# A two-layer hybrid encoder on one core: S5 parameters made once, the second layer's S5 tables moved into the first feed-forward stage, and reciprocal roots on GpSimd

## Chip, core and metric

One Trainium2 chip, one of its cores. The metric is the device time of one execution, in microseconds. TensorE multiplies matrices into PSUM; VectorE (DVE), ScalarE (ACT) and GpSimd (POOL) do elementwise work, each with its own in-order queue; SyncE (SP) and ScalarE issue the transfers.

## The reference, cut to what matters

The input is 512 positions of 1024 channels. Each of two layers runs three token mixers in parallel on the normalized input (differential attention with 8 heads, a 2-D Fourier mix, a bidirectional S5 state-space layer), gates and merges them, and goes on with a gated feed-forward of width 2816 and a gated per-layer embedding (PLE).

```python
def rms_norm(x, g):
    y = xf * lax.rsqrt(jnp.mean(xf * xf, axis=-1, keepdims=True) + EPS)
    return y * g
def s5_mix(u, a_re, a_im, log_dt, b_re, b_im, c_re, c_im, d):
    ...
    for direction in range(2):
        lam = lax.complex(a_re[direction], a_im[direction])
        dt = jnp.exp(log_dt[direction])[:, None]
        a_bar = jnp.exp(lam * dt)
        b_scale = (a_bar - 1.0) / lam
        _, xs = lax.associative_scan(_ssm_combine, (a_elems, bu * b_scale), axis=1,
                                     reverse=(direction == 1))
        state = state + xs
    y = jnp.einsum('bsgp,ghp->bsgh', state, c_mat).real
```

There are 32 S5 groups of 16 channels with 64 complex states each, and the parameters (a, dt, b, c) depend on the weights alone, not on x.

## The kernel before, in words

Activations lie with channels on the 128 partitions and all 512 positions in the free dimension, so a tile is 128x512. Each f32 product is made of three matmuls on split operands: `unit` loads 512 KB of weights (two buffers `wr`), ScalarE makes the high parts `wh` (line 94), VectorE the low parts `wl` by subtraction (line 95), six buffers each, and `mm` (line 106) runs high-high, high-low and low-high. A unit of 1024 columns gives 24 matmuls. Results go into the PSUM banks "w" (three), "s" (two), "t", "o" and "m" (one each).

The program is written as a list of tile operations; a planner orders them on each engine when the kernel is built. An operation written earlier goes first among those that are ready; `high_priority(offset=-LOW)` puts what is in it 600 places later. The order is then fixed, and each engine goes through its queue in order.

A layer runs: the norm; `s5_params`; `s5_load_u` (S5 input, stored to DRAM); `fourier`; eight heads of attention (v in pairs, q and k with rotary, `head`), with `s5_tables` for the eight chunks of four S5 groups written between the heads; `s5_toeplitz`; then the gather of U from DRAM, `s5_chunk` for eight chunks among the gates and branch projections, `s5_out`, the GLU, w_out; the norm and the feed-forward (22 pairs of units up, eight rows down); the norm and PLE.

`s5_params` (line 277 on) makes the powers of the discretized pole, the scaled inputs and the phase tables for one layer's 64 columns (2 directions x 32 groups); 144 instructions on VectorE and 24 on GpSimd, and leaves them in SBUF (Wr, Wi, BWr, BWi and phases). `s5_tables` makes from them, for one chunk: products `tb` on GpSimd (lines 400, 401, 417, 418, and complex products at lines 238 to 243), an addition on VectorE (402, 419), 16 matmuls with `cat` (410), two ScalarE copies behind each pair of them into `vbt` and `kfb` (411, 412), and six stores to the DRAM table `tab` (413, 420, 435, 438). Buffers are few: `tb1` has two, `tb2`, `bc` and `vbt` one. `s5_toeplitz` lays `kfb` out in the DRAM table `dtab`.

`rsqrt` (line 109) makes 1/sqrt by a bit trick and three Newton steps: eight small VectorE instructions on 128x4 values. It stands behind every norm and behind every head (`rms`), where a matmul with the result (line 146) follows.

Of the kernel before, what the change touches and what calls it, by code (L numbers as in the profile page):

```python
# [50 lines left out]
class Kernel:  # L51
# [57 lines left out]
    def rsqrt(self, pool, v, n):  # L109

        nc = self.nc
# [91 lines left out]
    def exp_acc(self, pool, out, x, n, V):  # L203
        k = self.t(pool, "ex1", (P, 64))[:, :n]
        r = self.t(pool, "ex2", (P, 64))[:, :n]
        q = self.t(pool, "ex3", (P, 64))[:, :n]
# [39 lines left out]
    def setup(self):  # L246
# [8 lines left out]
        nc.vector.memset(self.ones, 1.0)  # L255
        self.cst = self.t(self.cp, "cst", (P, 3))
# [17 lines left out]
    def s5_params(self, i, keep, pool, R):  # L274
        nc, a = self.nc, self.a
        V = nc.vector
        n = 64
# [5 lines left out]
        nc.sync.dma_start(prm, a["s5p"][i])  # L283
# [18 lines left out]
        Wr = self.t(keep, "Wr", (P, 8, n))  # L302
        Wi = self.t(keep, "Wi", (P, 8, n))
        Br = self.t(keep, "BWr", (P, 8, n))
        Bi = self.t(keep, "BWi", (P, 8, n))
        V.tensor_tensor(out=Wr[:, 0], in0=r1, in1=c, op=ALU.mult)
        V.tensor_tensor(out=Wi[:, 0], in0=r1, in1=sn, op=ALU.mult)
# [6 lines left out]
        V.tensor_scalar(out=nr, in0=Wr[:, 0], scalar1=-1.0, scalar2=None, op0=ALU.add)  # L314
        V.tensor_tensor(out=t, in0=nr, in1=are, op=ALU.mult)
        V.tensor_tensor(out=u, in0=Wi[:, 0], in1=aim, op=ALU.mult)
        V.tensor_tensor(out=t, in0=t, in1=u, op=ALU.add)
        V.tensor_tensor(out=Br[:, 0], in0=t, in1=den, op=ALU.mult)
        V.tensor_tensor(out=t, in0=Wi[:, 0], in1=are, op=ALU.mult)
        V.tensor_tensor(out=u, in0=nr, in1=aim, op=ALU.mult)  # L320
        V.tensor_tensor(out=t, in0=t, in1=u, op=ALU.subtract)
        V.tensor_tensor(out=Bi[:, 0], in0=t, in1=den, op=ALU.mult)

        tmp = self.t(pool, "ptmp", (P, 7, n))
        G = nc.gpsimd
        for w in (1, 2, 4):
            self.cmul(G, Wr[:, w:2 * w], Wi[:, w:2 * w], Wr[:, 0:w], Wi[:, 0:w],
                      Wr[:, w - 1:w].to_broadcast([P, w, n]), Wi[:, w - 1:w].to_broadcast([P, w, n]), tmp[:, 0:w])
        self.cmul(G, Br[:, 1:8], Bi[:, 1:8], Wr[:, 0:7], Wi[:, 0:7],
                  Br[:, 0:1].to_broadcast([P, 7, n]), Bi[:, 0:1].to_broadcast([P, 7, n]), tmp)  # L330
# [12 lines left out]

        ph = []
        for q in range(2):
            co = self.t(keep, f"phc{q}", (P, n, 8))
            si = self.t(keep, f"phs{q}", (P, n, 8))
            V.memset(co[:, :, 0:1], 1.0)
            V.memset(si[:, :, 0:1], 0.0)
            f = [c8, s8] if q == 0 else [fc, fs]  # L350
            k = 1
            while True:
                b = [P, n, k]
                self.cmul(V, co[:, :, k:2 * k], si[:, :, k:2 * k], co[:, :, 0:k], si[:, :, 0:k],
                          f[0].unsqueeze(2).to_broadcast(b), f[1].unsqueeze(2).to_broadcast(b),
                          tmp.rearrange("p k n -> p (k n)")[:, :n * k].rearrange("p (n k) -> p n k", k=k))
                k *= 2
                nf = [self.t(pool, f"pf{q}{k}c", (P, n)), self.t(pool, f"pf{q}{k}s", (P, n))]
# [5 lines left out]
                if k == 8:  # L364
                    break
            fc, fs = f
            ph.append((co, si))
# [3 lines left out]
        return dict(Wr=Wr, Wi=Wi, Br=Br, Bi=Bi, ph=ph)  # L371

    def s5_tables(self, i, pool, prm, ch, kfb, cat, tab, prio):
# [5 lines left out]
        nc.sync.dma_start(bc, a["s5bc"][i, ch])  # L379

# [7 lines left out]
        def wsel(w, d, rev):  # L388
            v = w.rearrange("p k (d g) -> p d g k", d=2)[:, d, g0:g0 + GC]
            if rev:  # L390
                v = v[:, :, ::-1]
            return v.unsqueeze(3).to_broadcast(full)
# [4 lines left out]
        for d in range(2):  # L397
            vb = self.t(pool, "tb1", full, bufs=2)
            t2 = self.t(pool, "tb2", full, bufs=1)
            G.tensor_tensor(out=vb, in0=wsel(prm["Br"], d, d == 0), in1=bsel(0), op=ALU.mult)  # L400
# [349 lines left out]
    def layer(self, i, x):  # L750
# [12 lines left out]
        self.xp.release()  # L763

        self.op = self.pool(f"o{i}", side="right")
        gp = self.pool(f"gen{i}", side="right")
        rp = self.pool(f"r{i}")
        cosr = self.t(rp, "cosr")
        sinr = self.t(rp, "sinr")
# [450 lines left out]
```

## Time and profile before

| what | value |
|---|---|
| median of 3 runs | 2235.33 us (2235.26 to 2237.52) |
| the profiled execution's own time | 2237.99 us |
| its span, first to last instruction | 2236.2 us |
| mean granted TensorE clock | 0.983 |
| TensorE matmul busy | 2121.7 us (95%) |
| VectorE busy | 1534.3 us (69%) |
| ScalarE busy | 1023.5 us (46%) |
| GpSimd busy | 760.2 us (34%) |

Busy time is the union of an engine's instructions. Matmuls are pipelined, and their ends are modelled, so a busy TensorE is not one at full pace. In time, layer 1's attention lies at about 110 to 446 us, its feed-forward at 720 to 1075 us, PLE to 1135 us; layer 2's Fourier part begins near 1150 us and its attention ends near 1546 us.

### The profile page before, as it was taken

Reading aid. Unit: us, or ns where it says so; the run is one execution under the profiler, and the core shown is the slowest. Engines: PE = TensorE matmul, PEld = TensorE weight load, DVE = VectorE, ACT = ScalarE, POOL = GpSimd, SP = SyncE. Lnnn points to the kernel's source line nnn. Section 1 sums busy time; section 2 is a strip of 40 time slices with the busy share of each in tenths; the row PEclk is TensorE's granted clock in tenths of the full one; section 3 lists DMA queues with packets and bytes.
Section 4 is the critical chain, followed back from the end, with each engine's and each line's share of the span. In section 5 each row is a group of like instructions: output and inputs, shape, how many; then the busy total and the mean of one; then the engine's idle time right before and its main releaser. Section 6 shows DMA issues by size and latency. Waiting matters only on the chain.

```text
span 2236.2 us, 29074 instructions
## 1 busy us (share of the span) xinstructions
PE 2121.7 (95%) x10432; PEld 1772.2 (79%) x10432; DVE 1534.3 (69%) x2664; ACT 1023.5 (46%) x1900; POOL 760.2 (34%) x748
## 2 busy tenths in 40 slices
PE   7888989899999999999998898898999999999998
PEld 5777778688888888888887787687888888888886
DVE  7988997566666766633689899984666667665344
ACT  4256665244434444433442766552445444444333
POOL 4497876223101322200025967841330012221000
PEclk9999999999999999999998999999999999999999
DMA  5232232665323333233432322236743323333341
GB/s 186 79 110 78 86 101 97 190 222 197 116 94 95 97 102 95 92 95 97 149 118 80 105 87 90 97 123 186 259 150 107 97 90 101 97 95 96 95 130 57
DMA packets 117232, 259.20 MB, mean 116 GB/s; under 512 B 43456, under 2 KB 49856, under 8 KB 115040
## 3 DMA queue, kind: packets, MB, share of 16 engines
q1 hardware_dynamic: 87040, 218.48, 31.3%
q10 hardware_dynamic: 30048, 38.87, 5.2%
q8 instruction: 82, 1.34, 0.3%
q14 instruction: 62, 0.51, 0.1%
HBM read 216.87 MB, written 40.37 MB: 115 GB/s over the span
## 4 chain that ended last, share of the span: by engine, by line
PE 69%; DVE 13%; POOL 6%; DMA 5%; ACT 3%; issue 2%; ACTq 0%; SPq 0%; DVEq 0%; POOLq 0%
PE w L106 55%; PE s L106 5%; DVE wl L95 2%; DMA tab<-tb 1%; PE s L639 1%; DVE mx L541 1%; DMA U<-usd 1%; PE w L1079 1%; POOL ra L501 1%; POOL tb L417 1%; DVE tb L402 1%; DVE pr L553 1%; PE w L1026 1%; PE w L1028 1%; PE w L1027 1%
## 5 line engine op out<-in xcount | busy, mean ns | idle before, releaser
L95 DVE TENSOR_TENSOR wl<-wr,wh 128x512 fp32r<-128x512 f32 x596 | 465.5, 785 | 303.5 <-ACT wh L94 295.6
L94 ACT ACTIVATE wh<-wr 128x512 fp32r<-128x512 f32 x596 | 368.5, 624 | 631.4 <-PE w L106 424.7
L106 PE MATMUL w<-hh,wh 128*128 128x512 f32 x1536 | 607.8, 396 | 20.1 <-DVE rs L499 9.0
L106 PE MATMUL w<-hl,wh 128*128 128x512 f32 x1536 | 604.8, 394 | 2.3 <-DVE hl L82 2.2
L106 PE MATMUL w<-hh,wl 128*128 128x512 f32 x1536 | 604.6, 394 | 1.6 <-DVE wl L95 1.6
L106 PEld LDWEIGHTS w<-hh,wh 128*128 128x128 f32 x1536 | 291.6, 190 | 82.5 <-DVE rs L499 10.6
L106 PEld LDWEIGHTS w<-hl,wh 128*128 128x128 f32 x1536 | 291.2, 190 | 63.5 <-DVE hl L82 5.0
L106 PEld LDWEIGHTS w<-hh,wl 128*128 128x128 f32 x1536 | 290.9, 189 | 62.0 <-DVE wl L95 2.2
L180 POOL TENSOR_TENSOR sq<-sq,sq 128x512 f32<-128x512 f32 x18 | 25.0, 1391 | 454.0 <-ACT sq L178 454.0
L191 POOL TENSOR_TENSOR ge<-ge,cv 128x512 f32<-128x512 f32 x44 | 57.8, 1315 | 305.3 <-DVE ge L190 305.3
L106 PE MATMUL w<-ah,wl 128*128 128x512 f32 x352 | 140.4, 399 | 0.0
L106 PE MATMUL w<-al,wh 128*128 128x512 f32 x352 | 138.7, 394 | 0.0
L106 PE MATMUL w<-ah,wh 128*128 128x512 f32 x352 | 138.0, 392 | 0.0
L546 ACT ACTIVATE pr<-s,mx 128x512 f32<-128x512 f32 x128 | 87.9, 689 | 54.5 <-DVE mx L541 49.2
L541 DVE TENSOR_REDUCE mx<-s 128x1 f32<-128x512 f32 x128 | 85.7, 678 | 8.9 <-PE s L540 8.9
L936 POOL TENSOR_TENSOR uu<-uu,cv 128x512 f32<-128x512 f32 x44 | 58.2, 1323 | 71.9 <-DVE cv L193 71.9
L106 PEld LDWEIGHTS w<-al,wh 128*128 128x128 f32 x352 | 66.1, 188 | 17.1
L539 PE MATMUL s<-ks,qs 128*128 128x512 f32 x128 | 56.9, 450 | 23.7 <-ACT pr L546 23.0
L106 PEld LDWEIGHTS w<-ah,wh 128*128 128x128 f32 x352 | 66.1, 188 | 15.8
L106 PEld LDWEIGHTS w<-ah,wl 128*128 128x128 f32 x352 | 66.1, 188 | 15.3
L106 PE MATMUL w<-oh,wh 128*128 128x512 f32 x128 | 52.6, 421 | 14.8 <-DVE m L841 6.5
L553 DVE SCALAR_TENSOR_TENSOR pr<-pr,c,pr 128x512 f32<-128x512 f32 x64 | 65.8, 1028 | 1.0
(417 smaller groups left out, 4227.3 us busy)
## 6 DMA issues: line engine op xcount, KB each, us to landing
wr<-in_w_in SPq DMA_DIRECT2D x112, 512.0 KB
wr<-in_w_up SPq DMA_DIRECT2D x88, 512.0 KB
tb<-tab SPq DMA_DIRECT2D x16, 1536.0 KB
tab<-tb ACTq DMA_DIRECT2D x64, 256.0 KB
wr<-in_w_down SPq DMA_DIRECT2D x32, 512.0 KB
tab<-vbt ACTq DMA_DIRECT2D x32, 256.0 KB
wr<-in_w_attn SPq DMA_DIRECT2D x16, 512.0 KB
wr<-in_w_glu SPq DMA_DIRECT2D x16, 512.0 KB
```

Of the source, the lines that this page charges most:

```text
L94: nc.scalar.activation(hi[:, :n], raw[:, c:c + n], AF.Copy)
L95: nc.vector.tensor_tensor(out=lo[:, :n], in0=raw[:, c:c + n], in1=hi[:, :n].bitcast(F32), op=ALU.subtract)
L106: nc.tensor.matmul(ps, lhsT=w[i][a], rhs=b[i], start=start and i == 0 and q == 0, stop=stop and i == n - 1 and q == 2)
L180: eng.tensor_tensor(out=sq, in0=sq, in1=acc[c], op=ALU.add)
L191: nc.gpsimd.tensor_tensor(out=sq, in0=sq, in1=y, op=ALU.mult)
L402: nc.vector.tensor_tensor(out=vb, in0=vb, in1=t2, op=ALU.add)
L417: G.tensor_tensor(out=ct, in0=wsel(prm["Wr"], d, d == 1), in1=bsel(2), op=ALU.mult)
L539: nc.tensor.matmul(s, lhsT=q[:, c, qs], rhs=kk[:, c], start=True, stop=False)
L541: V.tensor_reduce(mx[:, c:c + 1], s, op=ALU.max, axis=AX.X, negate=True)
L546: nc.scalar.activation(pt, ss[c], AF.Exp, bias=mx[:, c:c + 1], accum_out=(s1, s2)[c][:, qt:qt + 1])
L553: V.scalar_tensor_tensor(out=pr[0], in0=pr[1], scalar=c2, in1=pr[0], op0=ALU.mult, op1=ALU.add)
L936: G.tensor_tensor(out=u, in0=u, in1=c, op=ALU.mult)
```

## The change

The parameters of both layers are made in one call, on 128 columns, in layer 1 only, behind `fourier` instead of ahead of `s5_load_u`. They no longer stay in SBUF: 16 transfers store them to the DRAM tile `par` (one piece per layer and chunk, 256 KB), and `s5_tables` loads its piece into a tile `pt` with one buffer. Layer 1's tables are written one chunk per head, 0 to 7 (before: 0 and 1 at the first head, then one ahead, none at the last). Layer 2's tables are written into the first layer's feed-forward, one chunk at each odd step 1 to 15, and its Toeplitz part behind the feed-forward. The transposed copies `vt` share the buffer of tag `tb2`. `rsqrt` becomes one GpSimd power of -0.5; the last norm of the output keeps the steps under the name `rsqrt_steps`. The host hands over the parameters in a new column order.

```diff
     def rsqrt(self, pool, v, n):
 
+        y = self.t(pool, "rsq", (P, 4), bufs=4)[:, :n]
+        self.nc.gpsimd.tensor_tensor(out=y, in0=v, in1=self.mhalf[:, :n], op=ALU.pow)
+        return y
+
+    def rsqrt_steps(self, pool, v, n):
+
...
-    def s5_params(self, i, keep, pool, R):
+    def s5_params(self, pool, R, par):
...
-        n = 64
+        n = 2 * NC
...
-        nc.sync.dma_start(prm, a["s5p"][i])
+        nc.sync.dma_start(prm, a["s5p"])
...
+        tab = self.t(pool, "ptab", (P, 8, n, 8))
+        Wr, Wi, Br, Bi = (tab[:, q] for q in range(4))
...
+        for q, v in ((0, w0r), (1, w0i), (2, b0r), (3, b0i)):
+            V.tensor_scalar(out=tab[:, q, :, 0], in0=v, scalar1=1.0, scalar2=None, op0=ALU.mult)
...
-        return dict(Wr=Wr, Wi=Wi, Br=Br, Bi=Bi, ph=ph)
-
-    def s5_tables(self, i, pool, prm, ch, kfb, cat, tab, prio):
+        for q in range(L * NCH):
+            nc.sync.dma_start(par[q], tab[:, :, q * 2 * GC:(q + 1) * 2 * GC].rearrange("p k n x -> p k (n x)"))
+
+    def s5_tables(self, i, pool, ch, kfb, cat, tab, prio):
...
+        prm = self.t(pool, "pt", (P, 8, 2, GC, 8))
+        nc.sync.dma_start(prm.rearrange("p k d g x -> p k (d g x)"), self.par[i * NCH + ch])
...
-                vt = self.t(pool, "vbt", (P, GC, P), bufs=1)
+                vt = self.t(pool, "tb2", (P, GC, P), bufs=1)
...
+    def s5_step(self, i, ch):
+        pool, kfb, cat = self.gen
+        with self.tc.high_priority(offset=-LOW):
+            self.s5_tables(i, pool, ch, kfb, cat, self.tabs[ch], self.tc.tile_snap_priority() - LOW)
...
-        tp = self.pool(f"tmp{i}")
-        prm = self.s5_params(i, gp, tp, s5R)
         fd = self.t(self.dp, "fd", (P, 4, T))
         fp = self.pool(f"four{i}")
         self.s5_load_u(i, up, hh, hl, rb, usd)
         self.fourier(i, fp, hh, hl, rb, fd)
         fp.release()
-        tp.release()
         up.release()
+        if i == 0:
+            self.s5R = self.t(self.cp, "s5R", (P, 2 * NC))
+            self.par = self.t(self.dp, "par", (L * NCH, P, 8, 2 * GC * 8))
+            tp = self.pool(f"tmp{i}")
+            self.s5_params(tp, self.s5R, self.par)
+            tp.release()
+            self.s5_begin(0, "right")
...
-            with tc.high_priority(offset=-LOW):
-                for ch in ([0, 1] if h == 0 else [h + 1] if h < 7 else []):
-                    self.s5_tables(i, gp, prm, ch, kfb, cat, tabs[ch], tc.tile_snap_priority() - LOW)
+            if i == 0:
+                self.s5_step(0, h)
...
         hh, hl, rc, rb = self.norm(x, V_GFFN)
+        if i + 1 < L:
+            self.s5_begin(i + 1, "left")
...
+            if i + 1 < L and f % 2 and f < 2 * NCH:
+                self.s5_step(i + 1, f // 2)
...
         ff.release()
+        if i + 1 < L:
+            self.s5_end(i + 1)
```

`s5_begin` allocates the pool, `kfb`, `cat` and the DRAM tables, and fills the identity part of `cat`; `s5_end` calls `s5_toeplitz` and releases the pool.

## Rows read from the trace of the kernel before

**Rows 1.** Stretches: length, busy of PE, PEld, DVE, ACT, POOL, clock, DMA, GB/s
```profile
110.00:446.00 336.00, 300.06 (x1638) 253.71 (x1636) 274.61 (x474) 182.85 (x393) 227.82 (x226) 0.96 0.35 110
446.00:720.00 274.00, 273.27 (x1358) 229.31 (x1359) 172.44 (x254) 123.05 (x204) 46.96 (x44) 1.00 0.47 146
720.00:962.00 242.00, 242.00 (x1067) 199.95 (x1066) 162.03 (x245) 113.61 (x179) 57.99 (x44) 1.00 0.31 97
962.00:1075.00 113.00, 113.00 (x489) 91.09 (x487) 42.84 (x71) 37.22 (x63) 5.28 (x9) 1.00 0.35 104
1150.00:1200.00 50.00, 39.36 (x216) 34.92 (x215) 46.64 (x139) 11.22 (x31) 25.20 (x35) 0.86 0.25 82
1150.00:1546.00 396.00, 351.20 (x1952) 301.45 (x1950) 330.87 (x643) 199.90 (x438) 253.17 (x263) 0.96 0.34 107
```

**Rows 2.** Matmuls by line, 1150 to 1546 us: first, tables', last group
```profile
L106 PE MATMUL w<-hh,wh 128*128 128x512 f32 x218 | 88.0, 404 | 3.9 <-DVE rs L499 3.9
...
L410 PE MATMUL m<-cat,tb 128*128 128x144 f32 x128 | 21.9, 295 | 4.9 <-DVE tb L402 4.0 <-ACT kfb L412 0.9
...
L132 PE MATMUL t<-ones,osb 128*128 128x1 f32 x8 | 1.0, 229 | 0.0
```

**Rows 3.** Chain that ended last, in time: start, us, what, count of instructions
```profile
455.45 1.73 PE s L639 x16
...
719.53 353.64 PE w L106 x1543
...
1197.57 3.11 PE w L1079 x26
```

**Rows 4.** One VectorE product of the S5 parameters, layer 1 (ns min/median/max)
```profile
L288 DVE TENSOR_TENSOR p_li<-prm,p_dt x1: 218/218/218, 60.6 to 60.6; 128x64 f32<-128x64 f32 x1
```

**Rows 5.** VectorE on roots, 1150:1546: temporary nww, line 117, line 115
```profile
1150.00:1546.00 396.00, 22.39 (x48) 0.96 0.34 107
1150.00:1546.00 396.00, 3.46 (x8) 0.96 0.34 107
1150.00:1546.00 396.00, 3.83 (x8) 0.96 0.34 107
```

**Rows 6.** Table buffer: PE, PEld, DVE, POOL in 1150:1546; line 402's additions
```profile
1150.00:1546.00 396.00, 21.93 (x128) 19.49 (x128) 36.34 (x35) 159.37 (x168) 0.96 0.34 107
...
L402 DVE TENSOR_TENSOR tb<-tb,tb x32: 670/684/1783, 99.9 to 1487.7; 128x512 f32<-128x512 f32 x32
```

**Rows 7.** Timeline of ScalarE behind the gather of U, layer 1
```profile
446.02 1.15 ACT L94 ACTIVATE wh<-wr 128x512 fp32r<-128x512 f32 x2 [12.42 <-DMA U<-usd]
```

**Rows 8.** VectorE, line 95 alone: stretch, length, busy us (count), clock, DMA
```profile
110.00:446.00 336.00, 50.29 (x50) 0.96 0.35 110
...
720.00:962.00 242.00, 63.93 (x90) 1.00 0.31 97
```

**Rows 9.** First table product and last table step of chunks, layer 1
```profile
L400 POOL TENSOR_TENSOR tb<-BWr,bc x16: 1098/1558/1647, 85.0 to 383.1; 128x512 f32<-128x512 f32 x16
L437 POOL TENSOR_SCALAR tb<-tb,cst x8: 691/692/1075, 149.3 to 417.4; 128x512 f32<-128x512 f32 x8
```

**Rows 10.** Waits of 110 to 446 us: us in total, times, longest
```profile
ACT pr L546 <- DVE mx L541: 27.2, 21, 5.6
POOL tb L417 <- PE m L410: 25.5, 6, 6.9
...
POOL tb L417 <- DMA tab<-tb: 11.0, 5, 4.4
```

**Rows 11.** Layer 1's S5 results, GLU matmuls, gelu split: first, last start
```profile
L668 ACT ACTIVATE ye<-t x8: 365/384/386, 475.3 to 563.4; 128x256 f32<-128x256 f32 x8
...
L106 PE MATMUL s<-soh,wh x64: 387/394/398, 612.3 to 660.8; 128*128 128x512 f32 x64
...
L82 DVE SCALAR_TENSOR_TENSOR sol<-yg,soh x4: 1096/1097/1114, 579.5 to 602.1; 128x512 fp32r<-128x512 f32 x4
```

**Rows 12.** A small GpSimd instruction in the timeline
```profile
1319.34 0.24 POOL L384 TENSOR_SCALAR bc<-bc 128x64 f32<-128x64 f32 x1 [1.80 <-DMA bc<-in_s5bc]
```

More of the change, by code (lines that the diff above doesn't have):

```diff
@@ L301, in s5_params @@
         unit(c, sn)
[L302 to L307, printed above, removed]
+        tab = self.t(pool, "ptab", (P, 8, n, 8))
+        Wr, Wi, Br, Bi = (tab[:, q] for q in range(4))
+        w0r, w0i, b0r, b0i = s("w0r"), s("w0i"), s("b0r"), s("b0i")
+        V.tensor_tensor(out=w0r, in0=r1, in1=c, op=ALU.mult)
+        V.tensor_tensor(out=w0i, in0=r1, in1=sn, op=ALU.mult)
         den, nr = s("den"), s("nr")
@@ L342, in s5_params @@
         unit(c8, s8)
-        ph = []
+        f = [c8, s8]
+        tv = self.t(pool, "ptmv", (P, n, 4))
         for q in range(2):
-            co = self.t(keep, f"phc{q}", (P, n, 8))
-            si = self.t(keep, f"phs{q}", (P, n, 8))
+            co, si = tab[:, 4 + 2 * q], tab[:, 5 + 2 * q]
             V.memset(co[:, :, 0:1], 1.0)
             V.memset(si[:, :, 0:1], 0.0)
-            f = [c8, s8] if q == 0 else [fc, fs]
-            k = 1
-            while True:
+            for k in (1, 2, 4):
                 b = [P, n, k]
                 self.cmul(V, co[:, :, k:2 * k], si[:, :, k:2 * k], co[:, :, 0:k], si[:, :, 0:k],
[L355 to L358, printed above, removed]
+                          f[0].unsqueeze(2).to_broadcast(b), f[1].unsqueeze(2).to_broadcast(b), tv[:, :, 0:k])
+                nf = [self.t(pool, f"pf{k}c", (P, n)), self.t(pool, f"pf{k}s", (P, n))]
                 V.tensor_tensor(out=t, in0=f[0], in1=f[0], op=ALU.mult)
@@ L426, in s5_tables @@
         for d in range(2):
-            lo = [x.rearrange("p (d g) k -> p d g k", d=2)[:, d, g0:g0 + GC].unsqueeze(2).to_broadcast(full)
-                  for x in prm["ph"][0]]
-            hi = [x.rearrange("p (d g) k -> p d g k", d=2)[:, d, g0:g0 + GC].unsqueeze(3).to_broadcast(full)
-                  for x in prm["ph"][1]]
+            lo = [prm[:, q, d].unsqueeze(2).to_broadcast(full) for q in (4, 5)]
+            hi = [prm[:, q, d].unsqueeze(3).to_broadcast(full) for q in (6, 7)]
             t2 = self.t(pool, "tb2", (P, 512), bufs=1)[:, 0:256].rearrange("p (g a b) -> p g a b", g=GC, a=8)
@@ L438, in s5_tables, with s5_begin, s5_end @@
         nc.scalar.dma_start(tab[:, 2560:3072], si)
+    def s5_begin(self, i, side):
+        pool = self.pool(f"gen{i}", side=side)
+        kfb = self.t(pool, "kfb", (P, 2, NG, 16))
+        cat = self.t(pool, "cat", (P, GC, W1))
+        self.nc.scalar.activation(cat[:, :, :P], self.ident.unsqueeze(1).to_broadcast([P, GC, P]), AF.Copy)
+        self.tabs = [self.t(self.dp, f"tab{ch}", (P, 3072)) for ch in range(NCH)]
+        self.dtab = self.t(self.dp, "dtab", (P, 8, NG, 16))
+        self.gen = pool, kfb, cat
+    def s5_step(self, i, ch):
+        pool, kfb, cat = self.gen
+        with self.tc.high_priority(offset=-LOW):
+            self.s5_tables(i, pool, ch, kfb, cat, self.tabs[ch], self.tc.tile_snap_priority() - LOW)
+    def s5_end(self, i):
+        pool, kfb, _ = self.gen
+        self.s5_toeplitz(i, pool, kfb, self.dtab)
+        pool.release()
     def s5_toeplitz(self, i, pool, kfb, dtab):
@@ L780, in layer @@
         tp.release()
-        tabs = [self.t(self.dp, f"tab{ch}", (P, 3072)) for ch in range(NCH)]
-        dtab = self.t(self.dp, "dtab", (P, 8, NG, 16))
         usd = self.t(self.dp, "usd", (T, T))
         ysd = self.t(self.dp, "ysd", (P, NG * NC))
-        s5R = self.t(rp, "s5R", (P, 64))
-        tp = self.pool(f"tmp{i}")
-        prm = self.s5_params(i, gp, tp, s5R)
         fd = self.t(self.dp, "fd", (P, 4, T))
@@ L1047, in ple_last @@
                 V.scalar_tensor_tensor(out=evs[tt], in0=ss, scalar=1.0 / D, in1=evs[tt], op0=ALU.mult, op1=ALU.add)
-                rs = self.rsqrt(self.small, evs[tt], 1)
+                rs = self.rsqrt_steps(self.small, evs[tt], 1)
                 x0 = xt[:, tt, 0:512]
```

65 lines of the change are left out of this document (29 added, 36 removed).

## The prediction

> **What bounds the kernel now.** I read the busy times stage by stage first. From 446 to 1075 us TensorE is busy almost without a break, with VectorE at 63 and 67% and then 38% [rows 1]; there only TensorE's own work counts. In the attention of both layers it is otherwise: 110 to 446 us and 1150 to 1546 us, where VectorE is busy 275 of 336 and 331 of 396 us, and TensorE has pauses [rows 1].
>
> "Busy" hides part of the pauses, so I count TensorE's work in layer 2's stretch. The list of matmuls by line for 1150 to 1546 us has 29 groups, of which the first, the last and the tables' own stand here [rows 2]; by columns they are 892 of 512, 636 of 256 or 258, 128 of 144 and 296 of 128 or fewer. Where nothing stops TensorE, the chain of waits gives 353.64/1543 = 229 ns for 512 columns, 3.11/26 = 120 ns for 256 and 1.73/16 = 108 ns for 64 [rows 3]; I put 144 columns between the last two, at 115 ns. Full pace: 204 + 76 + 15 + 32 = 327 us. So of 396 us 69 are stall. The same stretch has a granted clock of 0.96, and of 0.86 in its first 50 us [rows 1]: a part of the 69 us is half clock behind pauses. That is what a lighter VectorE can give back in layer 2.
>
> **Layer 2's attention: what leaves it.** Three VectorE loads go.
> The S5 parameters: 144 VectorE instructions by my count of the function, most near the 218 ns of a 128x64 product [rows 4], some longer beside GpSimd; 144 x 0.24 = 35 us, crowded into the 50 us in which VectorE is busy 46.6 [rows 1].
> The reciprocal roots: eight heads of eight instructions. Six of the eight go by one temporary, 48 instructions in 22.4 us; the two others take 3.8 and 3.5 us [rows 5]; together 30 us.
> The tables: 32 additions. The rows of the table buffer show 35 instructions in 36.3 us, of which three belong to the S5 stage [rows 6]; 34 us.
> Sum 99 us: VectorE falls from 331 to about 232 us. Tables on GpSimd go too (159 us of 253) and 128 matmuls (15 us).
>
> TensorE's floor becomes 327 - 15 = 312 us. How much stall stays? If the share of stall (69 of 396) stayed, the stretch would take 312/0.83 = 377 us, a gain of 19; with none, 312, a gain of 84. VectorE would be at 232/334 = 69%, nearest to the rows at 63 and 67% without pauses, so I take a value near the lower stall, 22 us: among it the gather of U, which held ScalarE for 12.4 us in layer 1 and which nothing in the diff touches [rows 7]. Layer 2: 396 - 334 = **62 us saved**.
>
> **The first feed-forward stage: what enters it.** TensorE has no pause there, so its 128 matmuls (15 us) are paid in full. The rest must fit beside the feed-forward work: GpSimd 159 us, VectorE 34 us, 32 pairs of ScalarE copies, per chunk two loads and six stores, and at the end the 15 stores that lay out the Toeplitz part, with ScalarE at 114 of 242 us [rows 1]. Over 720 to 1075 us GpSimd has 63 us of its own work [rows 1], so the room is there, 355 us for 159.
> VectorE is the doubtful one. A weight subtraction took 63.93/90 = 0.71 us here and 50.29/50 = 1.01 us in layer 1's attention, where GpSimd was busy 68% of the time [rows 1, 8]. If the tables were all made before 962 us, the 90 subtractions would take 27 us more, 66 other two-input instructions perhaps 10, so 162 + 34 + 37 = 233 of 257 us, 91%, more than the 84% that went with 17% of stall in layer 2's attention. That is the upper bound: 17% of 257 = 44 us. The lower is 0. The code splits weights up to three units (6 high and 6 low buffers, 24 matmuls or 5.5 us a unit) ahead of TensorE and has three banks, which attention's score chain lacks, and tables may run on below 962 us, where VectorE is at 38%. I take 7. **22 us lost.**
> The Trainium skill, page "GPSIMD Engine Reference", section "Key points", says that GpSimd shares its SBUF interfaces with VectorE and that instructions with two SBUF inputs contend with it. By that rule the FFN's subtractions would slow towards attention's 1.01 us and the sum would move towards the 44 us; taking the FFN's own 0.71 us it stays at 0. The trace agrees as far as those two rows go.
>
> **Layer 1.** Here nothing leaves but the roots. It has 30 us less VectorE work on its 275; at layer 2's rate (62 us for 99 us of VectorE and 15 of TensorE) that would be worth 15 us. But the order of the tables changes, and they decide when S5 can end.
> Before, the parameters ran beside the Fourier work, the first table product started at 85.0 us, chunks ended from 149.3 to 417.4 us, one each 38.3 us, back to back [rows 9]: a chain that waits for itself (25.5 us for its matmuls to free a buffer, 11.0 us for a store [rows 10]), not for the heads. After it came the S5 chunks (last result 563.4 us), the gelu splits (last at 602.1) and the GLU matmuls from 612.3 us [rows 11]: a margin of 10 us, with other matmuls filling until then.
> After: the parameters stand behind Fourier, in memory that Fourier uses. One row of 128 columns instead of 64 costs (670 - 218)/448 = 1.0 ns a column more, 65 ns [rows 4, 6], so 144 x 65 ns = 9 us, phases and copies some 8 more: 35 + 17 = 52 us of VectorE in one chain, drawn out to some 65 us by attention's own instructions between. I set Fourier's end at about 80 us: the first table product stood at 85.0 while Fourier and the parameters shared VectorE [rows 9]. Then come 16 stores and a load through DRAM, two waits of about 3 us (11.0/5 = 2.2 us was the mean wait for a store [rows 10]). 80 + 65 + 6: I put the first table product at 150 us.
> Per chunk, the parameter tile has one buffer and its last reader is the chunk's last step, so the next load (some 3 us) stands open; and the transposed copies now share the scratch buffer of the second product, so the next second product waits for matmuls, copies and store, for which 25.5/6 = 4.3 us was the mean wait [rows 10]; I put 5 us. Period 38.3 + 8 = 46 us. Eight chunks: 150 + 370 = 520, less some 20 when the heads have ended and the engines are free: 500, some 80 us later than 417.
> What of that reaches the end? Before, the chunks had to wait for U until 446 us, 28 us after the last table; that wait lies beside the tables now. About 55 us remain. The S5 stage itself took 446 to 563 us, sharing transfers at 146 GB/s with weights [rows 1]; with two table loads and their first half done ahead I take 25 us off. 55 - 25 - 10 of margin = **20 us lost**. Lower bound: chain hidden, relief paid, 15 gained; upper: nothing made up but the margin, 70 lost.
> The 16 stores go through SP's queue, which also brings the weights: 16 of 256 KB in 256-byte pieces. Weights behind them wait; three split units (16 us) cover it, without them up to the 20 us that I already count.
>
> **The power operation.** No row has one. Nearest is a GpSimd instruction of 128x64 at 0.24 us [rows 12]; above I set the 3.7 us of a chain that it replaces (30/8). Eight heads: 2 to 30 us of GpSimd, on the 94 us or fewer that are left in layer 2 [rows 1, 6], so nothing; in layer 1 it stands among the table products in GpSimd's queue: 0 to 30 us within the upper bound above. I take 0.3 us. It makes GpSimd wait for VectorE's variance, with rotary and table products queued behind it, whose matmuls then wait; VectorE's own queue is free of it. The norms ahead of feed-forward and PLE lie in stretches without pauses: nothing. The last root keeps its steps.
> Of the small edits (one load of parameters instead of two, roots of one buffer, the column order on the host) none lies on a path that sets the end: nothing.
>
> **Sum.** -62 + 22 + 20 = -20 us on the profiled execution's 2238.0 (its span is 2236.2): 2218. That execution lies 2.7 us above the median, so on the median 2235.3 it is **2215 us**.
>
> **Rivals.**
> A, as summed: 2215, chance 0.46, own range 2195 to 2230.
> B, layer 1's tables are hidden: gates and two projections after attention are long enough, and the relief pays 15 us. 2235 - 62 + 22 - 15 = 2180. For it: VectorE and GpSimd are free after 446 us [rows 1]; against it the 10 us of margin. 0.22.
> C, the other side: layer 1's GLU waits for its tables. Place: the first GLU matmul, 612.3 us before. Each us later costs one; from 40 us later the gains are gone. At 70, 2235 - 62 + 22 + 70 = 2265. For it the back-to-back chain; against it that chunks after attention run faster. 0.14.
> D, contention in the feed-forward stage: 44 us in place of 7, 2252. VectorE is at 91%, and late table products hold the in-order queues of VectorE and TensorE [rows 8]; the rule above says the same. Against it the three units of lead. 0.09.
> E, the change doesn't free layer 2: heads are bound by their own chain of scores, maximum, exponential and transposes, and only 19 us come back. 2258. For it, the exponential's wait for the maximum, 27.2 us in layer 1 [rows 10]; against it, VectorE makes the maximum, and it is VectorE that is freed. 0.09.
>
> **Range and chances.** About 0.2% (4.5 us) is what a measurement tells from none. Faster: B and nearly all of A (0.43), 0.65; within: 0.06, half from A's upper edge and half from milder forms of D and E; slower: the rest of C, D and E, 0.29. The range leaves out half of C and the outer ends of B, D and E, 0.2 in all: 2170 to 2262.
>
> **What would show it.** Right: 1150 to 1546 us shrinks to about 335 with VectorE near 70%; 720 to 1075 grows by 15 to 25 us; layer 1's GLU starts 10 to 40 us later than 612 with a pause of TensorE ahead of it. Wrong: a GLU start before 612 (B) or after 650 (C); subtractions near 1 us and pauses in the feed-forward stage (D); pauses in layer 2's heads as before (E).

## The result and the profile after

The change made the kernel slower: 2349.29 us (median of 4 runs, 2344.51 to 2351.04) against 2236.07 us for the kernel before beside it, a ratio of 1.0502 (95% interval 1.0484 to 1.052). The profiled execution took 2344.51 us, with a span of 2342.6 us; before, the span was 2236.2. So 106 us are to be found.

The page's busy times of the changed kernel: engine, us, share, instructions.

```profile
PE 2126.8 (91%) x10432; PEld 1777.9 (76%) x10432; DVE 1481.8 (63%) x2349; ACT 1016.6 (43%) x1895; POOL 778.8 (33%) x746
```

TensorE is busy 5 us longer than before (2121.7), and VectorE has 52 us less to do. So 101 of the 106 us are pauses of TensorE. A count by landmarks says where they lie (first GLU matmul, first result of the up half, first and last matmul of the down half, layer 2's first GLU matmul):

| stretch | before | after | change |
|---|---|---|---|
| start to layer 1's GLU | 612 | 732 | +120 |
| GLU and w_out to the up half | 107 | 106 | -1 |
| up half of feed-forward 1 | 224 | 258 | +34 |
| down half | 122 | 129 | +7 |
| down half to layer 2's GLU | 648 | 595 | -53 |
| layer 2's GLU to the end | 523 | 523 | 0 |

The feed-forward's 41 us and layer 2's 53 leave a gain of 12. Layer 1 loses 120. Such a landmark is good to some 7 us: the profiled execution was the fastest of its four, and in four runs below that leave layer 1 as it is in the changed kernel, layer 1's GLU starts at 734.7 to 739.2 us, not at 732.2.

Stretches of the changed kernel, columns as in [rows 1]: layer 1's start, the end of its tables behind the heads, the up and down halves, PLE and layer 2 up to its heads, and layer 2's heads.

```profile
110.00:150.00 40.00, 0.11 (x1) 0.14 (x1) 39.23 (x77) 0.00 (x0) 17.21 (x11) 0.50 0.00 1
...
503.00:550.00 47.00, 22.18 (x79) 17.33 (x80) 10.43 (x14) 4.43 (x13) 19.17 (x26) 0.64 0.66 169
838.00:1096.00 258.00, 241.67 (x1074) 199.64 (x1073) 210.04 (x250) 109.43 (x207) 160.44 (x141) 0.97 0.38 116
1096.00:1225.00 129.00, 127.91 (x566) 103.09 (x565) 57.61 (x78) 38.46 (x78) 58.95 (x67) 1.00 0.45 138
1225.00:1414.00 189.00, 174.73 (x913) 149.44 (x912) 114.30 (x195) 84.02 (x164) 52.55 (x54) 0.95 0.41 130
1414.00:1622.00 208.00, 202.48 (x1171) 174.62 (x1170) 160.68 (x306) 139.47 (x277) 54.72 (x39) 1.00 0.19 59
```

The first row is the surprise: for 40 us VectorE works without a break (39.23 us), GpSimd for 17.21 us, and TensorE does nothing. After the heads (second row) every engine is half idle or more, and the granted clock falls to 0.64. The last row is what the change was to do: layer 2's heads at 97% of TensorE (202.48 of 208) with VectorE at 77%.

Waits of the changed kernel from 85 to 175 us: who waited for what, us in all, times, longest.

```profile
ACT vh L81 <- DMA par<-ptab: 73.8, 1, 73.8
...
PE w L106 <- DVE rs L522: 58.6, 1, 58.6
POOL kz L825 <- DMA par<-ptab: 42.5, 1, 42.5
...
DVE vl L82 <- DMA pt<-par: 20.8, 1, 20.8
...
PE w L106 <- DVE vl L82: 14.6, 1, 14.6
```

Two things hold attention here, and TensorE pauses 58.6 + 14.6 us. From the timelines of VectorE and ScalarE:

```profile
147.80 0.69 DVE L249 TENSOR_TENSOR ptab<-ptab,ptmv 128x512 f32<-128x512 f32 x1
148.41 0.68 DVE L521 TENSOR_TENSOR ra<-w,cosr 128x512 f32<-128x512 f32 x1
...
170.06 0.47 ACT L81 ACTIVATE vh<-w,rsq 128x256 fp32r<-128x256 f32 x1 [73.78 <-DMA par<-ptab]
```

The pause of 58.6 us ends when VectorE comes to the first rotary steps (`ra`, then `rs`), right behind the last step of the parameters: VectorE's queue was full of the parameters until then, and the stores had only begun. Attention's own first tiles, `vh` and `kz`, wait longer, until 170 us, for a store of the parameters. Nothing in the computation links them. They lie in the memory that the parameters' pool has just given back, so they can be written only when the last of the 16 stores has read `ptab`. That costs TensorE the 14.6 us (for `vl` the profile names the load behind the stores), and the first table product stands behind `kz` in GpSimd's queue.

The tables of layer 1 in the changed kernel, by source line (ns min/median/max, first and last start): first product, last step of the chunks (the stretch up to 700 us alone), the stores, the power operation; and layer 1's GLU matmuls.

```profile
L405 POOL TENSOR_TENSOR tb<-pt,bc x32: 1044/1058/1585, 172.3 to 1207.7; 128x512 f32<-128x512 f32 x32
...
L440 POOL TENSOR_SCALAR tb<-tb,cst x8: 694/697/1011, 232.6 to 553.7; 128x512 f32<-128x512 f32 x8
...
L374 SPq DMA_DIRECT2D par<-ptab x16: 623/1158/1203, 148.6 to 165.3; - x16
...
L112 POOL TENSOR_TENSOR rsq<-rmv,mhalf x22: 1008/1022/1560, 32.2 to 2285.3; 128x4 f32<-128x4 f32 x22
...
L106 PE MATMUL s<-soh,wh x64: 387/394/398, 732.2 to 780.6; 128*128 128x512 f32 x64
```

Against [rows 9, 11]: the first product at 172.3 and not 85.0, the last chunk's end at 553.7 and not 417.4, the GLU at 732.2 and not 612.3. The period of a chunk is (553.7 - 232.6)/7 = 45.9 us; it was 38.3.

### The profile page after: what moved, and what is told of

Same layout as the page of the kernel before. It is cut to its first block, busy times and chain, and to the rows that moved or that the text cites. A ratio compares the mean times of both kernels' runs of the same rounds, so it can differ in the third digit from the quotient of the medians.

```text
span 2342.6 us, 28753 instructions
## 1 busy us (share of the span) xinstructions
PE 2126.8 (91%) x10432; PEld 1777.9 (76%) x10432; DVE 1481.8 (63%) x2349; ACT 1016.6 (43%) x1895; POOL 778.8 (33%) x746
## 4 chain that ended last, share of the span: by engine, by line
PE 65%; DVE 11%; POOL 10%; DMA 6%; ACT 4%; issue 3%; SPq 1%; ACTq 1%; POOLq 0%; DVEq 0%
PE w L106 47%; PE s L106 4%; DMA tab<-tb 2%; PE w L1103 2%; PE o L586 1%; DMA fraw<-fd 1%; DVE wl L95 1%; POOL ge L197 1%; PE m L415 1%; PE s L662 1%; POOL uu L956 1%; POOL tb L244 1%; PE s L562 1%; POOL tb L247 1%; PE s L563 1%
## 5 line engine op out<-in xcount | busy, mean ns | idle before, releaser
L95 DVE TENSOR_TENSOR wl<-wr,wh 128x512 fp32r<-128x512 f32 x596 | 475.4, 803 | 269.3 <-ACT wh L94 257.2
L415 PE MATMUL m<-cat,tb 128*128 128x144 f32 x256 | 48.2, 315 | 47.5 <-DVE tb L407 45.2
L523 POOL TENSOR_TENSOR rs<-rs,sinr 128x512 f32<-128x512 f32 x32 | 47.2, 1475 | 116.7 <-DVE rs L522 101.9
L415 PEld LDWEIGHTS m<-cat,tb 128*128 128x128 f32 x256 | 41.1, 206 | 57.1 <-issue 37.0
L956 POOL TENSOR_TENSOR uu<-uu,cv 128x512 f32<-128x512 f32 x44 | 64.0, 1456 | 50.0 <-DVE cv L199 50.0
L422 POOL TENSOR_TENSOR tb<-pt,cat 128x512 f32<-128x512 f32 x32 | 36.7, 1147 | 126.7 <-PE m L415 118.4
```

What stands on the lines that cost most here:

```text
L95: nc.vector.tensor_tensor(out=lo[:, :n], in0=raw[:, c:c + n], in1=hi[:, :n].bitcast(F32), op=ALU.subtract)
L415: nc.tensor.matmul(pv[:, q], lhsT=vbf[:, g + q], rhs=cat[:, g + q], start=True, stop=True)
L422: G.tensor_tensor(out=ct, in0=wsel(0, d, d == 1), in1=bsel(2), op=ALU.mult)
L523: nc.gpsimd.tensor_tensor(out=rs, in0=rs, in1=sinr, op=ALU.mult)
L956: G.tensor_tensor(out=u, in0=u, in1=c, op=ALU.mult)
```

## The experiments

Three theories stood at the start. The memory theory: the 73 us in which TensorE stands still near 91 to 165 us are lost for good. The chain theory: only the end of the last table counts, and the GLU follows it by a fixed distance, whatever happens before. The third: VectorE's 63 us of work on the parameters are the price, wherever they stand. Each run is given with the time of the kernel before on the same chip as a ratio.

**The parameters' pool on the other side of memory**, so that attention's pools don't follow it.

```diff
-            tp = self.pool(f"tmp{i}")
+            tp = self.pool(f"tmp{i}", side="right")
```

> The parameters' working memory lies on the other side of the memory, where attention's tiles do not follow it; order in the text and arithmetic are unchanged. Theory 1 (attention's tiles wait for the memory of the parameters, so TensorE stands still from 91 to 165 us): the pause goes, 2349 falls to 2275 to 2300 us. Theory 2 (layer 1's GLU waits for the chain of tables, whatever starts attention): the pause goes but reappears ahead of GLU, 2325 to 2345 us. Theory 3 (the 63 us of VectorE work of the parameters are themselves the price): a pause of some 50 us stays at another place, within 10 us of 2349.

Measured: 2313.33 us, ratio 1.0345 (1.033 to 1.0361), 36 us less than the change. Both pauses are gone, and yet the GLU starts only 33 us earlier, at 699. The last table ends at 526.5, 27 us earlier:

```profile
L440 POOL TENSOR_SCALAR tb<-tb,cst x8: 694/700/1532, 208.4 to 526.5; 128x512 f32<-128x512 f32 x8
...
L106 PE MATMUL s<-soh,wh x64: 387/394/398, 699.5 to 747.9; 128*128 128x512 f32 x64
```

The edit did a second thing. On the other side the parameters no longer wait for Fourier's memory either. Their first instruction and their stores, in this run and then the first instruction in the changed kernel:

```profile
L358 DVE MEMSET ptab<- x2: 165/165/165, 1.0 to 1.4; 128x128 f32 x2
L374 SPq DMA_DIRECT2D par<-ptab x16: 619/1164/2254, 124.4 to 141.4; - x16
```

```profile
L358 DVE MEMSET ptab<- x2: 165/165/165, 85.1 to 85.6; 128x128 f32 x2
```

The parameters now run beside Fourier, and their stores begin 24 us earlier. So the run does not tell which of the two removed the pause of 58.6 us. Against the third theory, VectorE does the same work on the parameters here, and 36 us are back.

**The parameters written ahead of the S5 input and Fourier** (the call moves up; Fourier's and S5's pools lie behind it).

> The parameters are made ahead of the S5 input and Fourier, as before the change, still for both layers and still through DRAM. Theory 1: the pause at 91 to 165 us shrinks to under 20, 2270 to 2300 us. Theory 2: the first table product comes at 110 to 125 us in place of 172, chunk 8 ends 50 us earlier and GLU with it, 2285 to 2310 us, and the pause ahead of GLU stays near 40 us. Theory 3: VectorE's 63 us now delay Fourier, no better than 2335 us.

Measured: 2330.32 us, ratio 1.0423 (1.0407 to 1.0438). The first table product starts at 152.8, as early as with the other memory, but chunks still take 46.4 us, the last ends at 538 and the GLU starts at 716. All three forecasts missed: TensorE still pauses 18.1 + 15.2 us where the memory theory had under 20, the first product is 28 us later than the chain theory had it, and the time is 5 us under the third theory's 2335. What holds is that the last table and the GLU both come 16 us earlier.

**The transposed copies in a buffer of their own**, in layer 1 only.

```diff
-                vt = self.t(pool, "tb2", (P, GC, P), bufs=1)
+                vt = self.t(pool, "tb2" if i else "vbt", (P, GC, P), bufs=1)
```

> In layer 1 alone the transposed copies have their own buffer again, as before the change; in layer 2 they still share it, for want of memory. Theory 2 (the chain of tables ends layer 1): period of a chunk in layer 1 from 46 us back to 38 to 41, last table 35 to 55 us earlier, 2300 to 2330 us. Theory 1: attention, not the tables, sets layer 1's time; period shrinks, but the time falls by less than 10 us.

Measured: 2291.98 us, ratio 1.0252 (1.0234 to 1.0271): the largest gain of one edit, 57 us, by one buffer of 2 KB a partition. Its last tables and layer 1's GLU, a wait from 85 to 230 us, and a wait of GpSimd in the whole span, of this run and then of the changed kernel:

```profile
L440 POOL TENSOR_SCALAR tb<-tb,cst x8: 695/1012/1535, 210.9 to 497.2; 128x512 f32<-128x512 f32 x8
...
L106 PE MATMUL s<-soh,wh x64: 387/394/398, 675.5 to 723.9; 128*128 128x512 f32 x64
```

```profile
PE w L106 <- DVE rs L522: 58.6, 1, 58.6
```

```profile
POOL tb L422 <- PE m L415: 74.4, 16, 12.0
```

```profile
POOL tb L422 <- PE m L415: 118.4, 24, 12.0
```

The pause is untouched at 58.6 us. What shrank is GpSimd's wait for the transposing matmuls: 118.4 us in 24 waits in the changed kernel, 74.4 in 16 here (layer 2 still shares the buffer). The first product starts at 172.4 as before the edit, the period is 40.9, the last table 497.2 (57 us earlier) and the GLU 675.5 (57 us earlier). This run and the first one part the theories: the first removes the whole pause and leaves the period of a chunk (45.4 us) while the chain starts 22 us earlier, this one keeps the pause and shortens the period, and in both the GLU moves by what the last table moves, within 6 us.

**The roots by steps again**, all else as changed.

```diff
-        rc = self.rsqrt(self.small, v, 4)
+        rc = self.rsqrt_steps(self.small, v, 4)
```

> All reciprocal roots are made by the eight VectorE steps again; the rest is the changed kernel. If the power operation (1.02 us on GpSimd) relieves VectorE in both attentions, this run is 10 to 30 us slower than 2349. If its wait in GpSimd's queue holds rotary and table products, this run is 5 to 20 us faster. If neither decides, within 5 us.

Measured: 2344.96 us, ratio 1.0482 (1.0464 to 1.0499). The intervals overlap: within the changed kernel the power operation costs or gives nothing that can be measured.

**The chain shortened everywhere**: the other memory, the own buffer, two buffers for `pt` in layer 1, and the eight stores of layer 2's parameters on ScalarE's queue.

> Layer 1 alone: own buffer for the transposed copies, two buffers for the loaded parameters, the parameters' memory on the other side, and the stores of layer 2's half of the parameters on ScalarE's queue. Theory 2 (layer 1's GLU starts some 175 us after the last table): the gains add up, last table at 450 to 470 us against 554, GLU at 625 to 645 us against 732, time 2240 to 2262 us. Theory 1 (memory taken over by attention): not faster than the run with the memory moved less 15 us, 2295 to 2313 us. By either the feed-forward stays 41 us longer than before.

Measured: 2257.01 us, ratio 1.0085 (1.0068 to 1.0102). First product 159.4, last table 471.1, GLU 646.8. Here 92 us of the 113 are back. The first and the third run gave 36 and 57 us, 93 together, so the second buffer and the other queue add nothing that shows. The period is 39.0 us, as good as before (38.3), but the chain starts 74 us later than before: its last table ends 54 us and the GLU starts 34 us later.

**Layer 2's tables back in layer 2's attention**, from `par`.

> Layer 2's tables are made in layer 2's attention again, from the stored parameters; all else as in the changed kernel. If the tables are what slowed the feed-forward, first up result to last down matmul falls from 387 back to 346 us. From there to layer 2's GLU: if the tables are what left layer 2's attention, 595 grows to 640 to 670 us and the time is 2350 to 2385; if the parameters and roots were what counted, it stays below 615 us and the time is 2320 to 2335.

Measured: 2404.39 us, ratio 1.0749 (1.0733 to 1.0765). The feed-forward is back at 225 + 122 us, but layer 2 takes 692 us from the down half to its GLU: 44 more than in the kernel before, although it no longer makes its parameters, and more than the 640 to 670 expected. Its last steps of chunks, and the same step in the kernel before:

```profile
L440 POOL TENSOR_SCALAR tb<-tb,cst x8: 694/695/1010, 1364.2 to 1705.3; 128x512 f32<-128x512 f32 x8
```

```profile
L437 POOL TENSOR_SCALAR tb<-tb,cst x8: 686/692/1127, 1252.6 to 1517.1; 128x512 f32<-128x512 f32 x8
```

The period is 48.7 us against 37.8. The GLU starts at 1880, 175 us after the last table, as in layer 1; in the kernel before it was 196 in layer 2 and 195 in layer 1. So layer 2's attention, too, is timed by the chain of its tables when they stand in it, and not by the load of VectorE.

**Layer 2's tables without their matmuls.**

```diff
+                if i:
+                    G.memset(kfb[:, d, g0:g0 + GC], 0.0)
+                    nc.scalar.dma_start(tab[:, d * 512:(d + 1) * 512], vb.rearrange("p g j h -> p (g j h)"))
+                    continue
```

> Layer 2's tables leave out the 128 matmuls of the transposition and of the Toeplitz part, their copies and the waits behind them (the untransposed product is stored in their place, and the Toeplitz input is zero). If the feed-forward's 41 us are the matmuls (15 us) and TensorE's wait for late products, it falls from 387 to 346 to 352 us. If they are VectorE slowed by GpSimd, it only falls by the 15, to 370 to 375 us. Layer 1 stays as it is.

Measured: 2350.02 us, ratio 1.0505 (1.0487 to 1.0523), no gain, and up and down halves of 270 + 123 us: both expectations missed. TensorE's waits in the up half (852 to 1122 us), first of this run, then of the changed kernel (838 to 1096):

```profile
PE w L106 <- DVE gp L948: 16.3, 10, 4.4
PE w L106 <- DVE uu L959: 15.2, 8, 4.5
```

```profile
PE m L415 <- DVE tb L407: 16.3, 4, 4.8
```

With the matmuls, TensorE waited for the tables' own additions, held in order by them. Without the matmuls nothing holds the products back, the tables take 34 us a chunk, GpSimd is busy 203 of 270 us, and it is now the feed-forward's own VectorE results that come late. The equal time hides a loss and a gain: the denser tables also cost 12 us between the GLU and the up half (118 us for 106), and since they end at 1058 and not at 1253, the stretch from the down half to layer 2's GLU takes 578 us, 17 less.

**The power operation alone, on the kernel before.**

> The kernel before with one edit: the power operation on GpSimd in place of the steps. If it relieves VectorE, layer 1's and layer 2's GLU start 5 to 15 us earlier each, 2205 to 2228 us. If the chain of tables sets both, GpSimd's 1.02 us a head and the wait lengthen it, 2236 to 2250 us.

Measured: 2225.11 us, ratio 0.9952 (0.9933 to 0.9971). It is a gain by itself, 11 us by the medians. The profiled execution was the slowest of its four (2233.02; the others took 2224.29 to 2225.84) and shows only 5 us: layer 1's GLU starts at 603.6, 9 us earlier, behind a last table that ends 9 us earlier (408.2), and 4 us are lost again between the down half and layer 2's GLU (652 us for 648). So where the rest of the 11 us lies, no trace shows.

**Table matmuls of layer 2 at low priority.**

```diff
-            with self.tc.high_priority(offset=self.tc.tile_snap_priority() - prio):
+            with self.tc.high_priority(offset=0 if i else self.tc.tile_snap_priority() - prio):
```

> The changed kernel, with one edit: in the first feed-forward stage the 128 table matmuls and their copies keep the low priority of the rest of the tables' work (600 places later); in layer 1 they are as they were. The changed kernel lost 34 us in the up half (224 to 258 us). Queue theory: TensorE, in order, was held by table matmuls whose VectorE addition was late (16.3 us in 4 waits on the addition of line 407); with the matmuls placed later these waits go, the up half takes 240 to 244 us and the kernel 2331 to 2336 us (ratio 1.043). Density theory: VectorE is slowed by the GpSimd products beside it, the feed-forward's own results are late in any case; the up half stays at 254 to 262 us and the time at 2344 to 2353 us. Third: the later matmuls hold the shared scratch buffer longer, the eight chunks take over 45.9 us each, the tables end after 1253 us and PLE waits for them: up to 15 us slower.

Measured: 2393.59 us, ratio 1.07 (1.0683 to 1.0717). The up half is 241 us, as the queue theory had it, and the wait for additions there 7.7 us. But the tables run on until 1304, and the stretch from the down half to layer 2's GLU grows from 595 to 656 us. TensorE's waits of this run from 1214 to 1330 us:

```profile
PE m L415 <- DVE tb L407: 43.2, 4, 20.6
PE w L106 <- DVE pg L1003: 12.9, 1, 12.9
```

The hold went where it is dearer: up half 17 us shorter, this stretch 61 us longer. (Another 7 us of the run lie ahead of layer 1's GLU, which the edit doesn't touch.) The up half was also relieved of a quarter of GpSimd's work (117 us against 160), so its 241 us don't prove the queue theory by themselves.

**Layer 2's additions on GpSimd.**

```diff
-            nc.vector.tensor_tensor(out=vb, in0=vb, in1=t2, op=ALU.add)
+            (G if i else nc.vector).tensor_tensor(out=vb, in0=vb, in1=t2, op=ALU.add)
```

and the same for `ct`.

> The changed kernel, with one edit: in layer 2's tables (made in the first feed-forward stage) the 32 additions of lines 407 and 424 run on GpSimd in place of VectorE. VectorE loses some 30 us of work in that stage, GpSimd gains 32 x 1.5 = 48 us. If what hurts the stage is the load of VectorE, the up half falls from 258 to 240 to 246 us and the kernel to about 2335 us. If it is GpSimd's two-input work beside VectorE that stretches VectorE's instructions, weight subtractions stay at 1.0 us or more, the up half stays at 256 to 264 us, the period per chunk grows by 6 us and PLE waits up to 40 us longer: 2350 to 2390 us.

Measured: 2360.72 us, ratio 1.056 (1.0541 to 1.0578). The up half stays at 260 us; the tables end at 1272, and PLE waits 17.7 us. Fewer instructions on VectorE did not help. The weight subtractions alone in the up half, VectorE's busy time (count): power operation alone, low matmuls, the change, additions on GpSimd, no matmuls.

```profile
709.00:934.00 225.00, 58.76 (x82) 1.00 0.32 96
```

```profile
845.00:1086.00 241.00, 77.37 (x82) 0.99 0.36 109
```

```profile
838.00:1096.00 258.00, 83.28 (x81) 0.97 0.38 116
```

```profile
843.00:1103.00 260.00, 83.85 (x81) 0.97 0.36 112
```

```profile
852.00:1122.00 270.00, 87.49 (x81) 0.95 0.39 125
```

That is 0.72, 0.94, 1.03, 1.04 and 1.08 us for the same 128x512 subtraction, while GpSimd was busy 25, 49, 62, 71 and 75% of the stretch. It rises with GpSimd's share, and not with VectorE's number of instructions (234, 243, 250, 231, 255). The Trainium skill, page "GPSIMD Engine Reference", section "Key points", says that the two engines share their SBUF interfaces and that instructions with two SBUF inputs contend; the five rows agree. They are five stretches that differ in more than GpSimd's share, so the cause is supported and not isolated.

**A version meant to beat both**: layer 1 as before (parameters of 64 columns in SBUF, own buffer, chunks one head ahead), the power operation, layer 2's tables in the feed-forward, and layer 2's parameters by themselves behind layer 1's last table. The edit cut to the lines that place them:

```diff
+            tp = self.pool("tmp1", side="right")
+            with tc.high_priority(offset=-LOW):
+                self.s5_params(1, tp, tp, self.s5R[:, NC:])
```

> Layer 1 as in the kernel before (parameters of 64 columns ahead of the Fourier work, kept in SBUF, chunks 0 and 1 at the first head, transposed copies in a buffer of their own), with the power operation; layer 2's parameters made by themselves behind layer 1's last table, in three stores to DRAM, and layer 2's tables in the first feed-forward stage as in the changed kernel. By the theory that the chain of layer 1's tables cost all of the loss: layer 1's GLU starts at 604 to 612 us as with the power operation alone, 41 us lost in the feed-forward, 53 to 58 us gained from there to layer 2's GLU; 2225 - 14 = 2211 us, ratio 0.985 to 0.993. Rival: layer 2's parameters (50 us of VectorE) cost TensorE time wherever they stand; 20 us of pause between 450 and 720 us, 2231 us, no gain over the power operation alone.

Measured: 2257.38 us, ratio 1.0091 (1.0077 to 1.0105). The last table ends at 407.3, yet the GLU starts at 645: the parameters stand in front of the S5 chunks, VectorE is busy 40.6 us of 450 to 500, and TensorE 30.3.

**The same with the parameters behind the last S5 chunk.**

> As the run with the parameters apart, but layer 2's parameters stand behind layer 1's last S5 chunk (from about 560 us) and not behind its last table (414 us); temporaries of theirs share memory. That run lost 41 us to the power operation alone before layer 1's GLU (645 against 604 us), with VectorE on the parameters from 443 to 475 us and TensorE busy 30 of the 50 us from 450 to 500. If the place did it, the GLU starts at 600 to 610 us, GLU and up half grow by 0 to 10 us together, and with 41 us lost in the feed-forward and 53 to 58 gained behind it the time is 2208 to 2222 us, ratio 0.985 to 0.993. If the parameters cost it wherever they stand, the stretch from the last S5 chunk to the feed-forward grows by 20 to 40 us: 2231 to 2255 us.

Measured: 2233.64 us (11 runs), ratio 0.9989 (0.998 to 0.9998). The GLU is back at 605, but the stretch from there to the up half takes 125 us and not 106. The stretch from 600 to 650 us of this run, columns as in [rows 1], and TensorE's longest wait between 550 and 720:

```profile
600.00:650.00 50.00, 35.54 (x145) 27.82 (x144) 48.14 (x143) 17.72 (x30) 16.42 (x24) 0.86 0.31 108
```

```profile
PE s L106 <- ACT t L921: 13.4, 2, 12.3
```

VectorE is full (48.14 of 50) and the GLU's gates queue behind parameters. The feed-forward costs 253 + 132 us, 38 more than with the power operation alone; from there to layer 2's GLU it is 595. This version is the kernel before's equal within 0.2%, 8.5 us slower than the power operation alone, which stays the best of all that ran.

## Why the prediction was wrong

The forecast was 2215 us; measured were 2349, outside the range. By its own steps:

**Layer 1: the step that failed.** The term was 20 us lost; it measured 120. The mechanism, tables that come late and set the GLU, was right (rival C, priced at 70); its size was not, in two places.

First, the last table: I put 500, 83 us later than before, and it was 553.7, 136 us later. The start of the first product was set at 150 and was 172.3. Of its three terms, Fourier's end was put at 80, and the parameters' first step on their data stands at 87.0; the 65 us of the parameters took 62 (last step until 148.5); the 6 us for 16 stores and a load took 24. The stores held SP's queue until the load could be issued, at 166.5, and the first product stood behind attention's `kz`, which waited for them in memory that I hadn't seen attention would take over. (The first experiment's 150.5 equals the forecast by another route: there, too, 26 us lie between the first store and the first product, but the parameters no longer wait for Fourier's memory.) The chunks took 553.7 - 172.3 = 381 us; I had 370, less 20 for the freed engines. The period was right (46 put, 45.9 measured), the 20 us were not there: with the heads ended, the chain still waited for itself, and TensorE's granted clock was 0.64. TensorE's longest waits of 503 to 575 us in the changed kernel:

```profile
PE m L415 <- DVE tb L407: 16.2, 2, 11.7
```

Second, the credits. From a lateness of 83 us I took 63: the wait for U (28), S5 chunks that run faster (25) and the margin (10). Measured are 16. The gather of U, the first product that needs the Toeplitz part and the last S5 results, after the change, and then the first two before:

```profile
L636 ACTq DMA_DIRECT2D U<-usd x8: 444/498/1128, 536.5 to 540.7; - x8
L685 PE MATMUL t<-U,dr x64: 217/275/475, 584.2 to 681.7; 128*128 128x64 f32 x64
L691 ACT ACTIVATE ye<-t x8: 363/384/386, 589.6 to 682.4; 128x256 f32<-128x256 f32 x8
```

```profile
L613 ACTq DMA_DIRECT2D U<-usd x8: 342/1156/2493, 433.0 to 443.5; - x8
L662 PE MATMUL t<-U,dr x64: 217/275/276, 457.0 to 562.7; 128*128 128x64 f32 x64
```

U is gathered ahead of the last table now, as I had it. But a second path stood beside that wait: the Toeplitz part is laid out through DRAM behind the last table, and its first product came 30 us after that table's last step, for 40 before. So 9 us came of the 28. From there to the last S5 result it took 98 us, for 106: 8 of the 25. From the last result to the GLU it took 50, for 49: nothing of the 10. In the first, third and fifth experiments the first Toeplitz product stands 24, 25 and 24 us behind the last table, and in all of these runs the GLU follows that product by 148 to 155 us. From the last table to the GLU it had been 195 us; measured were 178 after the change and 173, 178 and 176 in those three, so just 17 to 22 could be pressed out. The third experiment shows it best: 57 us off the chain, 57 us off the GLU. The 54 us by which the last table came later than put and the 46 us of missing credits are the 100 us.

**The shared scratch buffer** I priced at 5 us a chunk of a period 8 us longer. Undoing it gave 57 us, 5.0 us a chunk off the period and the rest from the first chunk (232.6 - 172.3 = 60 us, against 38.5 with the own buffer). The price was right for the period; the 22 us of the first chunk were not in it.

**Feed-forward 1**: 22 us put, 41 measured. TensorE's busy time on the tables' matmuls in the changed kernel, up and down half, columns length, PE, PEld, clock, DMA, GB/s:

```profile
838.00:1096.00 258.00, 14.63 (x80) 13.00 (x80) 0.97 0.38 116
1096.00:1225.00 129.00, 6.75 (x40) 5.97 (x40) 1.00 0.45 138
```

The matmuls were put at 115 ns, 15 us in all; 120 of them took 21.4 us here, 178 ns each ([rows 6] had 21.9 us for all 128 before, 171 ns each, and I put a lower figure). That is all of the down half's 7 us. Of the up half's 34, 14.6 are matmuls, 16.3 the wait for the tables' additions, and 3 other. So contention was put at 7 and measured 19. Rival D's mechanism (late table products hold TensorE's queue) is what the trace shows; its price of 44 was too high. How much of the 19 the hold and the slower VectorE cost apart stays open: the run without the matmuls lost 46 us in the up half with no such hold, but with denser tables. The subtractions slowed to 1.03 us, attention's figure of before (1.01), and VectorE was at 81%, not 91.

**Layer 2**: 62 us put, 53 measured, heads at 77% of VectorE for 70 put. PLE's wait for the last tables took some of it: 9.2 us in one wait, with tables running until 1253 when the down half ended at 1225; the run without table matmuls, whose tables end by 1058, saves 70 us there. But the reason given was only half right. I laid the stall to VectorE's load. The run with the tables back in layer 2 had VectorE busy 159 of 280 us, without parameters or roots, and was 44 us slower than before. What binds a stretch with tables is their chain.

**The power operation**: 0.3 us put, 1.02 us measured for 128x4. I costed it at nothing, and in the changed kernel it is; on the kernel before it gives 11 us, with layer 1's GLU 9 us earlier. The roots' relief in layer 1 was put at up to 15 us, the lower bound of the layer 1 term, so that size is near. That the late chain hides it in the changed kernel fits the runs, and none shows it.

**What stays open.** Against the power operation alone, the last two versions are 32 and 8.5 us slower, and making layer 2's parameters cost them 41 and 21 us ahead of the feed-forward. So without that price, moving the tables and freeing layer 2's start of its parameters would be worth 9 to 13 us, an estimate from these differences that no run shows. Whether the parameters have a place that costs less is open; making them in the kernel's start together with layer 1's, in SBUF, was not tried. The new order of layer 1's chunks, one per head, was not run by itself either; with it and the chain mended the period was 39.0 us for 38.3, so little of the loss can lie there.

## What to carry to other kernels

When a chain of small steps on several engines paces a stage, cost a change by what it does to the chain's start and to its period times the number of turns, and check how far the stage's end really follows the chain's end before crediting slack: a wait that goes is worth nothing where a second path of the same length lies beside it. A pool that is released is a dependence: whatever is allocated next on that side waits for the last reader of the old tiles, stores to DRAM among them (here `vh` and `kz` until 170 us, and the parameters themselves until 85 us for Fourier's), so look what follows a moved pool as well as what precedes it. Work moved into a full stage is paid for there in the in-order queue of the full engine, and a bundle of edits should be timed one by one: here the smallest one was the only one shown to gain.

## What the runs showed of the hardware

A GpSimd power on 128x4 takes 1.02 us (1008 to 1560 ns, 22 instructions), four times the 0.24 us of the instruction in [rows 12], which has sixteen times the columns. VectorE's instructions of 128x128 took anything from 0.27 to 2.12 us while GpSimd multiplied the parameters' powers (106 to 126 us of the changed kernel):

```profile
113.56 0.28 DVE L349 TENSOR_TENSOR p_u<-p_s 128x128 f32<-128x128 f32 x1
...
121.81 1.91 DVE L306 TENSOR_SCALAR p_t<-p_t 128x128 f32<-128x128 f32 x1
```

The second of these has one tensor as input; the same line took 0.22 us at 97.27 us, before GpSimd began.

One store of 256 KB in 256-byte pieces held SP's queue for 1158 ns (median of 16), and the first load behind them was issued at 166.5 us, 18 us after the first store (148.6).
